# Last down-projection without an accumulator swap, a final norm that leaves GpSimd, and matmuls of the wide products chained in program order

## The chip, the cores and the metric

The kernel runs on one core of a Trainium2 chip. The metric is the device time of one execution in microseconds (us), the median over several runs. The engines are TensorE (PE for matmuls, PEld for the weight loads that precede them), VectorE (DVE), ScalarE (ACT), GpSimd (POOL) and SyncE (SP), which issues most of the transfers.

## What is computed

A decoder trunk of two mixer layers and two feed-forward layers on 256 tokens of width 2048, in float32, with a final RMSNorm. The part that the change touches most is the last feed-forward layer and the norm behind it:

```python
def conv_ffn(h, w_up, conv_w, w_down):
    up = h @ w_up
    g, u = jnp.split(up, [D_FF], axis=-1)      # D_FF = 5632
    g = causal_dwconv(g, conv_w)               # width 3
    return (jax.nn.silu(g) * u) @ w_down

...
    x = x + conv_ffn(h, ffn_w_up[l], ffn_conv_w[l], ffn_w_down[l])
return rmsnorm(x, norm_final)
```

Layer 0 has dilated attention beside a convolution module, layer 1 attention with forget gates; both end in an output projection that is added to x.

## The kernel before

**Weights.** Every product streams its weights through `stream` (lines 79 to 98): SP loads 1 MB into a `raw` buffer (three of them); ACT rounds a chunk of 128x1024 into `whi`, and DVE subtracts it from `raw` to give the remainder `wlo`. There are four `whi` and four `wlo` buffers. A product of float32 numbers is made of the products of rounded parts and remainders. One chunk holds two blocks of 128 rows of k for 512 columns.

**Wide products.** `panel_b` (line 100) gives 512 output features by 256 tokens: four PSUM banks, one for each 128 features (m), and for each block of k a matmul of `whi` with both parts of x side by side (512 columns, L111), then one of `wlo` with the main part (256 columns, L115). With `wide=False`, in layer 0's mixer, the first is split in two (L113, L114). All panels take their banks from the pool `pacc` of five in rotation; a pool `pms` of three ("misc") serves attention, norms and transposes. So a panel's first bank is free at its start, and its other three are those of the panel before, which DVE and ACT empty first: `whole` (L121, L123) for gate panels g, up panels u and q and k; `add_x` (L214, L215) where the product is added to x: ob (layer 0's output), d0 (first down-projection) and oc (layer 1's output).

**Order.** The program is emitted in one order, and a scheduler with a timeline of its own fixes each engine's instruction order: it takes what is ready in that timeline, by priority. In the order that it makes, a panel's matmuls mostly alternate between L111 and L115, with runs of L111 in places. `tc.high_priority` moves the casts and subtractions ahead.

**The last projection.** The second feed-forward layer goes in two groups of up panels (gi = 0 and 1). For gi = 0, `down1` (line 618) transposes x back to token rows (`x_back`) and adds its products with `panel_a` (`mm_a`, L127 to L129: three matmuls of 512 columns for each block of k). For gi = 1 it closes both PSUM pools and opens a pool `pl` of eight banks, one for each 512 columns i and token tile t:

```python
        ps_scope.close()
        pl = ctx.enter_context(tc.tile_pool(name="pl", bufs=1, space=bass.MemoryType.PSUM))
        acc = [[pl.tile([P, 512], F32, name=f"acc_e{i}{t}") for t in range(2)] for i in range(4)]
```

These tiles are called acc_e. Of its 20 blocks of k, the first 18 go to both token tiles alike; the last two are split, token tile 0 first, then token tile 1. After each token tile `finish_rows` (L660) adds the four banks to o (`add_o`, L616), squares on ACT (L664), sums, takes the reciprocal root (`rsqrt_cols`, L157 to L165), multiplies by the gain `gb` on POOL (L669), scales by the root on DVE (L673) and ACT (L675), and stores (L676).

Of the kernel before, what the change touches and what calls it, by code (L numbers as in the profile page):

```python
# [34 lines left out]

P_AG, P_Q, P_K, P_V, P_O = 2.4, 2.6, 2.6, 2.4, 3.4
ACT_TAPS = (1,)
AHEAD, BEHIND, TAIL = 400, 300, 60


@with_exitstack
def trunk(ctx, tc, a):
# [6 lines left out]
    ps_scope = ctx.enter_context(ExitStack())  # L49
    pacc = ps_scope.enter_context(tc.tile_pool(name="pacc", bufs=5, space=bass.MemoryType.PSUM))  # L50
    pms = ps_scope.enter_context(tc.tile_pool(name="pms", bufs=3, space=bass.MemoryType.PSUM))

    def misc(name):
        return pms.tile([P, 512], F32, tag="misc", name=name)
# [24 lines left out]
    def stream(src_of, nk, width, name, dk=4, room=None):  # L79

        half = KC * 512 // width
        for c in range(0, nk, dk * 512 // width):
            n = dk * 512 // width
            raw = wp.tile([P, 2 * KC * 512], F32, tag="raw", name=f"raw_{name}_{c}", bufs=3)
            rv = raw[:, :n * width].rearrange("p (k c) -> p k c", k=n)
            loads.append(nc.sync.dma_start(out=rv, in_=src_of(c, n)))
            for h in range(0, n, half):
                if room is None:
                    hi = wp.tile([P, half, width], F32R, tag="whi", name=f"whi_{name}_{c + h}")
                    lo = wp.tile([P, half, width], F32R, tag="wlo", name=f"wlo_{name}_{c + h}")  # L90
                else:
                    hi = room.tile([P, half, width], F32R, tag="gp", name=f"whi_{name}_{c + h}", bufs=2)
                    lo = room.tile([P, half, width], F32R, tag="cv", name=f"wlo_{name}_{c + h}", bufs=2)
                with tc.high_priority(offset=AHEAD):
                    S.copy(hi, rv[:, h:h + half, :])  # L95
                    last = V.tensor_tensor(out=lo, in0=rv[:, h:h + half, :], in1=hi.bitcast(F32), op=ALU.subtract)  # L96
                fill_in(last)
                yield list(range(c + h, c + h + half)), hi, lo

    def panel_b(src_of, x2, kts, name, order=(0, 1, 2, 3), dk=4, wide=True):  # L100

        acc = {m: pacc.tile([P, 512], F32, tag="acc", name=f"acc_{name}_{m}") for m in order}
        for ks, hi, lo in stream(src_of, len(kts), P * len(order), name, dk):
            for m in order:
                ms = slice(m * P, (m + 1) * P)
                for j, k in enumerate(ks):
                    x = x2(kts[k])
                    if wide:  # L110
                        PE.matmul(acc[m], hi[:, j, ms], x.rearrange("p a t -> p (a t)"), start=k == 0, stop=False)  # L111
                    else:
                        PE.matmul(acc[m][:, :T], hi[:, j, ms], x[:, 0, :], start=k == 0, stop=False)  # L113
                        PE.matmul(acc[m][:, :T], hi[:, j, ms], x[:, 1, :], start=False, stop=False)  # L114
                    PE.matmul(acc[m][:, :T], lo[:, j, ms], x[:, 0, :], start=False, stop=k == len(kts) - 1)  # L115
        return acc

    def whole(out, acc, name):
# [35 lines left out]
    def rsqrt_cols(ps, scale, name, n=2):  # L154

        v = wk.tile([P, n], F32, tag="rs_v", name=f"v_{name}")
        V.tensor_scalar(out=v, in0=ps, scalar1=scale, scalar2=EPS, op0=ALU.mult, op1=ALU.add)  # L157
        r = wk.tile([P, n], F32, tag="rs_r", name=f"r_{name}")
        S.activation(r, v, AF.Sqrt)
        V.reciprocal(out=r, in_=r)  # L160
        t = wk.tile([P, n], F32, tag="rs_t", name=f"t_{name}")
        V.tensor_tensor(out=t, in0=r, in1=r, op=ALU.mult)
        V.tensor_tensor(out=t, in0=t, in1=v, op=ALU.mult)
        V.tensor_scalar(out=t, in0=t, scalar1=-0.5, scalar2=1.5, op0=ALU.mult, op1=ALU.add)
        V.tensor_tensor(out=r, in0=r, in1=t, op=ALU.mult)  # L165
        return r
# [451 lines left out]
    def down1(gi, w_dn, k0, kts, g2, fp):  # L618
        if gi == 0:
# [28 lines left out]
        for i in range(4):  # L648
            for got in part(i, at, KC):
                for t in range(2):  # L650
                    rows(i, t, at, *got)
        at = n - KC
# [7 lines left out]
    def finish_rows(acc, t):  # L660
        for i in range(4):
            cs = slice(512 * i, 512 * (i + 1))
            add_o(acc[i][t], t, i)
            S.activation(junk[:, 512 * (i % 2):512 * (i % 2) + 512], o[:, t, cs], AF.Square, accum_out=fs[:, t, i:i + 1])  # L664
        V.reduce_sum(out=sf[:, t:t + 1], in_=fs[:, t, :], axis=AX.X)
        rf = rsqrt_cols(sf[:, t:t + 1], 1.0 / D, f"fin{t}", 1)
        for i in range(4):
            cs = slice(512 * i, 512 * (i + 1))
            G.tensor_tensor(out=o[:, t, cs], in0=o[:, t, cs], in1=gb[:, cs], op=ALU.mult)  # L669
        for i in range(4):  # L670
            cs = slice(512 * i, 512 * (i + 1))
            if i % 2 == 0:
                V.tensor_scalar(out=o[:, t, cs], in0=o[:, t, cs], scalar1=rf, scalar2=None, op0=ALU.mult)  # L673
            else:
                S.activation(o[:, t, cs], o[:, t, cs], AF.Copy, scale=rf)  # L675
            nc.sync.dma_start(out=a["out"][t * P:(t + 1) * P, cs], in_=o[:, t, cs])  # L676

    ffn(1, ssq2, down1)

# [60 lines left out]
```

## Time and profile before

| what | before |
|---|---|
| median of 3 runs | 2239.58 us (2237.7 to 2240.04) |
| the profiled execution's own time | 2240.73 us |
| its span, first to last instruction | 2238.9 us |
| mean granted TensorE clock | 0.996 of full speed |
| PE busy | 2213.6 us, 99% of the span |
| DVE, ACT, POOL busy | 1493.3, 1120.4, 26.0 us |
| moved by DMA | 414.08 MB, mean 185 GB/s |

Times in rows are in us from the span's start. A row of the timeline gives start, duration, engine, line, operation, the tile written and the tiles read; "x3" means three merged instructions, and brackets hold the idle time of the engine before it with what ended it. Matmuls overlap in their pipeline, so the distance between two starts is what a matmul costs, not its duration.

### The profile page before, as it was taken

The numbers are of one execution on the slowest core, as the hardware profiler recorded it, in microseconds if no ns is written. First come the engines' busy times: TensorE is split into PE (matmuls) and PEld (weight loads), VectorE is DVE, ScalarE is ACT, GpSimd is POOL, SyncE is SP. The second block draws the span as 40 slices with busy tenths as digits, with TensorE's granted clock in tenths as the row PEclk, the third lists the DMA queues.
The fourth block names the chain that finished last, engine by engine and source line by source line (L and its number), as shares of the span: only waits on it lengthen the run. The fifth ranks groups of instructions, "written<-read, shape, count | busy, mean of one in ns | idle before, by whom it ended". The sixth has DMA issues, their size and how long they took to land.

```text
span 2238.9 us, 31976 instructions
## 1 busy us (share of the span) xinstructions
PE 2213.6 (99%) x12778; PEld 1944.4 (87%) x12778; DVE 1493.3 (67%) x2280; ACT 1120.4 (50%) x1579; POOL 26.0 (1%) x58
## 2 busy tenths in 40 slices
PE   8999999999999999999999999999999999999997
PEld 8999988888888888888888888888888888888886
DVE  6999988767754577666655555677666644676644
ACT  6567665544443445444554554455544433454433
POOL 0000000000000000000000000000000000000001
PEclk9999999999999999999999999999999999999999
DMA  8544445555555555555544444555555555555453
GB/s 289 182 183 169 162 177 188 188 188 189 188 188 188 188 188 189 188 189 188 189 173 170 170 170 170 188 183 193 188 188 188 188 190 195 188 185 188 168 194 122
DMA packets 60806, 414.08 MB, mean 185 GB/s; under 512 B 7296, under 2 KB 8000, under 8 KB 12272
## 3 DMA queue, kind: packets, MB, share of 16 engines
q1 hardware_dynamic: 59904, 410.72, 51.2%
q8 instruction: 100, 1.64, 0.3%
q10 hardware_dynamic: 144, 1.05, 0.1%
q0 software_dynamic: 608, 0.26, 0.0%
q14 instruction: 50, 0.41, 0.0%
HBM read 409.84 MB, written 2.10 MB: 184 GB/s over the span
## 4 chain that ended last, share of the span: by engine, by line
PE 97%; DMA 1%; DVE 1%; ACT 0%; SPq 0%; issue 0%; ACTq 0%; DVEq 0%
PE acc_g L111 15%; PE acc_u L111 14%; PE acc_g L115 7%; PE acc_u L115 7%; PE acc_d L111 7%; PE acc_d L115 4%; PE acc_oc L111 3%; PE acc_k L111 3%; PE acc_q L111 3%; PE acc_q L115 2%; PE acc_k L115 2%; PE acc_d L127 2%; PE acc_d L129 2%; PE acc_v L128 2%; PE acc_v L129 2%; PE acc_v L127 2%
## 5 line engine op out<-in xcount | busy, mean ns | idle before, releaser
L111 PE MATMUL acc_g<-xs,whi_g 128*128 128x512 f32 x1408 | 493.0, 397 | 0.0
L111 PE MATMUL acc_u<-xs,whi_u 128*128 128x512 f32 x1408 | 481.9, 395 | 0.0
L115 PE MATMUL acc_g<-xs,wlo_g 128*128 128x256 f32 x1408 | 388.7, 280 | 0.0
L115 PE MATMUL acc_u<-xs,wlo_u 128*128 128x256 f32 x1408 | 370.0, 279 | 0.0
L96 DVE TENSOR_TENSOR wlo_g<-raw_g,whi_g 128x1024 fp32r<-128x1024 f32 x176 | 215.2, 1224 | 166.3 <-ACT whi_g L95 166.3
L111 PEld LDWEIGHTS acc_g<-xs,whi_g 128*128 128x128 f32 x1408 | 262.6, 188 | 60.5
L111 PEld LDWEIGHTS acc_u<-xs,whi_u 128*128 128x128 f32 x1408 | 260.1, 188 | 52.7
L95 ACT CAST whi_u<-raw_u 128x1024 fp32r<-128x1024 f32 x176 | 185.1, 1052 | 239.6 <-PE acc_u L111 122.0
L96 DVE TENSOR_TENSOR wlo_u<-raw_u,whi_u 128x1024 fp32r<-128x1024 f32 x176 | 213.3, 1222 | 116.2 <-ACT whi_u L95 116.2
L95 ACT CAST whi_g<-raw_g 128x1024 fp32r<-128x1024 f32 x176 | 184.9, 1052 | 198.3 <-PE acc_u L111 93.3
L96 DVE TENSOR_TENSOR wlo_d<-raw_d,whi_d 128x1024 fp32r<-128x1024 f32 x136 | 166.5, 1225 | 161.4 <-ACT whi_d L95 161.2
L115 PEld LDWEIGHTS acc_u<-xs,wlo_u 128*128 128x128 f32 x1408 | 265.0, 188 | 9.0
L115 PEld LDWEIGHTS acc_g<-xs,wlo_g 128*128 128x128 f32 x1408 | 265.6, 189 | 3.0 <-DVE wlo_g L96 0.2
L95 ACT CAST whi_d<-raw_d 128x1024 fp32r<-128x1024 f32 x136 | 143.0, 1051 | 207.2 <-PE acc_d L111 118.8
L111 PE MATMUL acc_d<-hp,whi_d 128*128 128x512 f32 x704 | 245.2, 394 | 0.0
L115 PE MATMUL acc_d<-hp,wlo_d 128*128 128x256 f32 x704 | 194.4, 283 | 0.0
L111 PEld LDWEIGHTS acc_d<-hp,whi_d 128*128 128x128 f32 x704 | 131.3, 188 | 28.8
L115 PEld LDWEIGHTS acc_d<-hp,wlo_d 128*128 128x128 f32 x704 | 132.4, 188 | 1.9
L115 PE MATMUL acc_q<-xs,wlo_q 128*128 128x256 f32 x384 | 106.0, 283 | 0.0
L115 PE MATMUL acc_k<-xs,wlo_k 128*128 128x256 f32 x384 | 105.8, 281 | 0.0
L111 PE MATMUL acc_q<-xs,whi_q 128*128 128x512 f32 x256 | 90.6, 396 | 0.0
L96 DVE TENSOR_TENSOR wlo_e<-raw_e,whi_e 128x1024 fp32r<-128x1024 f32 x40 | 48.9, 1225 | 60.4 <-ACT whi_e L95 60.4
(305 smaller groups left out, 4178.0 us busy)
## 6 DMA issues: line engine op xcount, KB each, us to landing
raw_g<-in_ffn_w_up SPq DMA_DIRECT2D x88, 1024.0 KB, 4.7
raw_u<-in_ffn_w_up SPq DMA_DIRECT2D x88, 1024.0 KB, 4.8
raw_d<-in_ffn_w_down SPq DMA_DIRECT2D x68, 1024.0 KB, 4.7
raw_q<-in_od_w_in SPq DMA_DIRECT2D x16, 1024.0 KB, 4.8
raw_k<-in_od_w_in SPq DMA_DIRECT2D x16, 1024.0 KB, 4.8
raw_v<-in_od_w_in SPq DMA_DIRECT2D x16, 1024.0 KB, 4.7
raw_oc<-in_od_w_out SPq DMA_DIRECT2D x16, 1024.0 KB, 4.8
raw_e<-in_ffn_w_down SPq DMA_DIRECT2D x16, 1024.0 KB, 4.8
```

The costliest lines, as they stand in the source:

```text
L95: S.copy(hi, rv[:, h:h + half, :])
L96: last = V.tensor_tensor(out=lo, in0=rv[:, h:h + half, :], in1=hi.bitcast(F32), op=ALU.subtract)
L111: PE.matmul(acc[m], hi[:, j, ms], x.rearrange("p a t -> p (a t)"), start=k == 0, stop=False)
L115: PE.matmul(acc[m][:, :T], lo[:, j, ms], x[:, 0, :], start=False, stop=k == len(kts) - 1)
L127: PE.matmul(o, xh, hi, start=first, stop=False)
L128: PE.matmul(o, xh, lo, start=False, stop=False)
L129: PE.matmul(o, xl, hi, start=False, stop=last)
```

## The change

1. The pools `pacc` and `pms` stay open to the end. The eight acc_e tiles come from them: three from "misc", five from `pacc`.
2. In the last projection the first 16 blocks of k go to both token tiles alike, and the last four are split by token tile. Their eight chunks must all stay in SBUF; buffers come from tiles that are dead by then (gate and conv tiles, one `hp` buffer, the four ordinary buffers, one `raw` buffer).
3. The final norm: after each 512 columns the sum is added, squared on ACT, and for three of four multiplied by `gb` on DVE instead of POOL; the fourth is multiplied by root and gain in one DVE instruction. In `rsqrt_cols` two DVE multiplications become one instruction when there is one column. The order of the four output blocks becomes 1, 0, 3, 2. The priority of `finish_rows` (`TAIL`) goes.
4. Each matmul of a wide product depends on the one before it (no semaphore, only order), through the whole kernel: `in_order`.

```diff
+    issued = [None]
+    def in_order(*args, **kw):
+        i = PE.matmul(*args, **kw).ins
+        if issued[0] is not None:
+            tc.add_manual_dep(i, issued[0].name, mybir.DependencyInfo(mybir.DependencyClass.NoSync, mybir.DependencyReason.DATA),
+                              reason="order of a product's matmuls")
+        issued[0] = i
...
+        mm = in_order if wide else PE.matmul
...
-        V.tensor_tensor(out=t, in0=r, in1=r, op=ALU.mult)
-        V.tensor_tensor(out=t, in0=t, in1=v, op=ALU.mult)
+        if n == 1:
+            V.scalar_tensor_tensor(out=t, in0=r, scalar=v, in1=r, op0=ALU.mult, op1=ALU.mult)
...
-        ps_scope.close()
-        pl = ctx.enter_context(tc.tile_pool(name="pl", bufs=1, space=bass.MemoryType.PSUM))
-        acc = [[pl.tile([P, 512], F32, name=f"acc_e{i}{t}") for t in range(2)] for i in range(4)]
+        acc = [[None, None] for i in range(4)]
+        for b, (i, t) in enumerate((i, t) for i in range(4) for t in range(2)):
+            acc[i][t] = misc(f"acc_e{i}{t}") if b < 3 else pacc.tile([P, 512], F32, tag="acc", name=f"acc_e{i}{t}")
...
-        last = [next(part(i, at, KC, room=fp if i > 1 else None)) for i in range(4)]
-        for t in range(2):
-            for i in range(4):
-                rows(i, t, at, *last[i])
-            with tc.high_priority(offset=TAIL * t):
-                finish_rows(acc, t)
+        rooms = [from_gate] * 2 + [from_hidden] + [from_weights] * 4 + [from_raw]
+        at = n - 4
+        last = [list(part(i, at, 4, room=lambda nm: rooms.pop(0)(nm))) for i in range(4)]
+        for t in range(2):
+            for i in range(4):
+                for got in last[i]:
+                    rows(i, t, at, *got)
+                add_o(acc[i][t], t, i)
+                cs = slice(512 * i, 512 * (i + 1))
+                S.activation(junk[:, 512 * (i % 2):512 * (i % 2) + 512], o[:, t, cs], AF.Square, accum_out=fs[:, t, i:i + 1])
+                if i < 3:
+                    V.tensor_tensor(out=o[:, t, cs], in0=o[:, t, cs], in1=gb[:, cs], op=ALU.mult)
+            V.reduce_sum(out=sf[:, t:t + 1], in_=fs[:, t, :], axis=AX.X)
+            rf = rsqrt_cols(sf[:, t:t + 1], 1.0 / D, f"fin{t}", 1)
+            for i in (1, 0, 3, 2):
+                cs = slice(512 * i, 512 * (i + 1))
+                if i == 3:
+                    V.scalar_tensor_tensor(out=o[:, t, cs], in0=o[:, t, cs], scalar=rf, in1=gb[:, cs], op0=ALU.mult, op1=ALU.mult)
+                elif i == 1:
+                    V.tensor_scalar(out=o[:, t, cs], in0=o[:, t, cs], scalar1=rf, scalar2=None, op0=ALU.mult)
+                else:
+                    S.activation(o[:, t, cs], o[:, t, cs], AF.Copy, scale=rf)
+                nc.sync.dma_start(out=a["out"][t * P:(t + 1) * P, cs], in_=o[:, t, cs])
```

`from_gate`, `from_hidden`, `from_weights` and `from_raw` are small new functions that each return a pair of views for `whi` and `wlo` in one of the buffers named under 2.

## Rows read from the trace of the kernel before

**Rows 1.** The page, busy time, share of the span and instructions of the engines.
```profile
PE 2213.6 (99%) x12778; PEld 1944.4 (87%) x12778; DVE 1493.3 (67%) x2280; ACT 1120.4 (50%) x1579; POOL 26.0 (1%) x58
```

**Rows 2.** Waits of PE over the span: total, times, longest.
```profile
...
PE bc_n L174 <- DVE dg_n L172: 2.0, 1, 2.0
PE acc_ob L111 <- DVE y L453: 1.4, 1, 1.4
```

**Rows 3.** Timeline of PE where the last projection begins.
```profile
2110.68 0.28 PE L115 MATMUL acc_u<-xs,wlo_u 128*128 128x256 f32 x1
2114.27 0.79 PE L127 MATMUL acc_e<-whi_e,hp 128*128 128x512 f32 x1 [3.32 <-DVE half_u L123]
...
2120.27 0.39 PE L129 MATMUL acc_e<-whi_e,hp 128*128 128x512 f32 x1
...
2120.96 0.39 PE L129 MATMUL acc_e<-whi_e,hp 128*128 128x512 f32 x1
```

**Rows 4.** Windows there: length, busy time by engine, then granted TensorE clock (PEclk), DMA.
```profile
2110.90:2114.20 3.30, 0.06 (x1) 0.00 (x0) 3.30 (x9) 2.21 (x5) 0.00 (x0) 0.86 0.25 104
2114.20:2118.00 3.80, 3.73 (x9) 2.96 (x10) 1.45 (x5) 1.89 (x3) 0.00 (x0) 0.50 0.73 276
```

**Rows 5.** Timeline of DVE before the last projection begins: third chunk of its weights.
```profile
2109.19 1.23 DVE L96 TENSOR_TENSOR wlo_e<-raw_e,whi_e 128x1024 fp32r<-128x1024 f32 x1 [1.55 <-ACT whi_e L95]
```

**Rows 6.** Timeline of PE, last matmul of token tile 0's first bank, and of all.
```profile
2217.09 0.39 PE L129 MATMUL acc_e<-whi_e,hp 128*128 128x512 f32 x1
...
2226.80 0.39 PE L129 MATMUL acc_e<-whi_e,hp 128*128 128x512 f32 x1
```

**Rows 7.** Timeline of DVE in the final norm.
```profile
2217.52 0.69 DVE L616 TENSOR_TENSOR o<-acc_e,o 128x512 f32<-128x512 f32 x1 [1.27 <-PE acc_e L129]
...
2225.24 1.20 DVE L162 TENSOR_TENSOR t_fin<-r_fin 128x1 f32<-128x1 f32 x1
...
2229.43 0.68 DVE L616 TENSOR_TENSOR o<-acc_e,o 128x512 f32<-128x512 f32 x1
...
2231.77 0.51 DVE L162 TENSOR_TENSOR t_fin<-r_fin 128x1 f32<-128x1 f32 x1
2232.31 0.16 DVE L163 TENSOR_TENSOR t_fin<-t_fin,v_fin 128x1 f32<-128x1 f32 x1
...
2232.96 0.88 DVE L673 TENSOR_SCALAR o<-o,r_fin 128x512 f32<-128x512 f32 x2
```

**Rows 8.** Timeline of POOL in the final norm.
```profile
2221.35 6.30 POOL L669 TENSOR_TENSOR o<-o,xT 128x512 f32<-128x512 f32 x5 [1.01 <-ACT xT L664]
```

**Rows 9.** Windows over one gate panel each, of layer 0 and of layer 1.
```profile
439.50:462.00 22.50, 22.50 (x130) 19.55 (x129) 13.85 (x21) 11.01 (x16) 0.00 (x0) 1.00 0.55 190
...
1886.90:1909.10 22.20, 22.20 (x130) 19.57 (x129) 11.06 (x12) 9.43 (x11) 0.00 (x0) 1.00 0.55 194
```

**Rows 10.** Timeline of PE inside an up panel of layer 1.
```profile
1606.11 0.40 PE L111 MATMUL acc_u<-xs,whi_u 128*128 128x512 f32 x1
...
1608.94 0.40 PE L111 MATMUL acc_u<-xs,whi_u 128*128 128x512 f32 x1
...
1609.29 1.11 PE L111 MATMUL acc_u<-xs,whi_u 128*128 128x512 f32 x4
```

**Rows 11.** Timeline of DVE in the same up panel.
```profile
1605.14 1.22 DVE L96 TENSOR_TENSOR wlo_u<-raw_u,whi_u 128x1024 fp32r<-128x1024 f32 x1
```

**Rows 12.** Timeline, PE's first matmul of an up panel, DVE emptying the gate panel's banks.
```profile
462.04 0.40 PE L111 MATMUL acc_u<-xs,whi_u 128*128 128x512 f32 x1
...
461.52 1.08 DVE L123 TENSOR_TENSOR gp<-acc_g,half_g 128x256 f32<-128x256 f32 x3
```

**Rows 13.** Timeline, PE's first matmul of the last ob panel, DVE emptying a bank before.
```profile
337.60 0.40 PE L111 MATMUL acc_ob<-y,whi_ob 128*128 128x512 f32 x1
...
342.14 0.41 DVE L215 TENSOR_TENSOR xT<-acc_ob,xT 128x256 f32<-128x256 f32 x1
```

**Rows 14.** Window behind PE's wait for dg_n, columns as in rows 4.
```profile
34.50:38.00 3.50, 3.50 (x16) 3.32 (x16) 3.50 (x6) 2.83 (x5) 0.00 (x0) 0.51 0.57 169
```

More of the change, by code (lines that the diff above doesn't have):

```diff
@@ L48, in trunk @@
     wk = ctx.enter_context(tc.tile_pool(name="wk", bufs=2))
-    ps_scope = ctx.enter_context(ExitStack())
-    pacc = ps_scope.enter_context(tc.tile_pool(name="pacc", bufs=5, space=bass.MemoryType.PSUM))
-    pms = ps_scope.enter_context(tc.tile_pool(name="pms", bufs=3, space=bass.MemoryType.PSUM))
+    pacc = ctx.enter_context(tc.tile_pool(name="pacc", bufs=5, space=bass.MemoryType.PSUM))
+    pms = ctx.enter_context(tc.tile_pool(name="pms", bufs=3, space=bass.MemoryType.PSUM))
     def misc(name):
@@ L91, in stream @@
                 else:
-                    hi = room.tile([P, half, width], F32R, tag="gp", name=f"whi_{name}_{c + h}", bufs=2)
-                    lo = room.tile([P, half, width], F32R, tag="cv", name=f"wlo_{name}_{c + h}", bufs=2)
+                    hi, lo = room(f"{name}_{c + h}")
                 with tc.high_priority(offset=AHEAD):
@@ L110, in panel_b @@
                     if wide:
-                        PE.matmul(acc[m], hi[:, j, ms], x.rearrange("p a t -> p (a t)"), start=k == 0, stop=False)
+                        mm(acc[m], hi[:, j, ms], x.rearrange("p a t -> p (a t)"), start=k == 0, stop=False)
                     else:
-                        PE.matmul(acc[m][:, :T], hi[:, j, ms], x[:, 0, :], start=k == 0, stop=False)
-                        PE.matmul(acc[m][:, :T], hi[:, j, ms], x[:, 1, :], start=False, stop=False)
-                    PE.matmul(acc[m][:, :T], lo[:, j, ms], x[:, 0, :], start=False, stop=k == len(kts) - 1)
+                        mm(acc[m][:, :T], hi[:, j, ms], x[:, 0, :], start=k == 0, stop=False)
+                        mm(acc[m][:, :T], hi[:, j, ms], x[:, 1, :], start=False, stop=False)
+                    mm(acc[m][:, :T], lo[:, j, ms], x[:, 0, :], start=False, stop=k == len(kts) - 1)
         return acc
@@ L161, in rsqrt_cols @@
         t = wk.tile([P, n], F32, tag="rs_t", name=f"t_{name}")
[L162 to L163 removed]
+        if n == 1:
+            V.scalar_tensor_tensor(out=t, in0=r, scalar=v, in1=r, op0=ALU.mult, op1=ALU.mult)
+        else:
+            V.tensor_tensor(out=t, in0=r, in1=r, op=ALU.mult)
+            V.tensor_tensor(out=t, in0=t, in1=v, op=ALU.mult)
         V.tensor_scalar(out=t, in0=t, scalar1=-0.5, scalar2=1.5, op0=ALU.mult, op1=ALU.add)
@@ L646, in down1, with from_gate, from_hidden @@
                         rows(i, t, at, *got)
-        at = n - 4
-        for i in range(4):
-            for got in part(i, at, KC):
-                for t in range(2):
-                    rows(i, t, at, *got)
-        at = n - KC
-        last = [next(part(i, at, KC, room=fp if i > 1 else None)) for i in range(4)]
+        def from_gate(nm):
+            return [fp.tile([P, KC, 512], F32R, tag=tag, name=f"{w}_{nm}", bufs=2) for tag, w in (("gp", "whi"), ("cv", "wlo"))]
+        def from_hidden(nm):
+            both = fp.tile([P, 4, 2, T], F32R, tag="hp", name=f"wboth_{nm}", bufs=6).rearrange("p a b t -> p (a b t)")
+            return [both[:, 1024 * h:1024 * (h + 1)].rearrange("p (k c) -> p k c", k=KC) for h in range(2)]
@@ new lines, in from_weights, with from_raw @@
+        def from_weights(nm):
+            return [wp.tile([P, KC, 512], F32R, tag=w, name=f"{w}_{nm}") for w in ("whi", "wlo")]
+        def from_raw(nm):
+            both = wp.tile([P, 2 * KC * 512], F32, tag="raw", name=f"wboth_{nm}", bufs=3).bitcast(F32R)
+            return [both[:, 1024 * h:1024 * (h + 1)].rearrange("p (k c) -> p k c", k=KC) for h in range(2)]
+        rooms = [from_gate] * 2 + [from_hidden] + [from_weights] * 4 + [from_raw]
+        at = n - 4
+        last = [list(part(i, at, 4, room=lambda nm: rooms.pop(0)(nm))) for i in range(4)]
```

20 lines of the change are left out of this document (2 added, 18 removed).

## The prediction, made before the changed kernel ran

> **What bounds the kernel now.** I read the page first: PE is busy for 99% of the span [rows 1], so another engine matters only where it makes PE wait, or behind PE's last matmul. The list of PE's waits comes next. It is short: besides a start-up wait and the two of [rows 2], its longest is the 3.32 us in front of the last projection [rows 3]. The windows show that this wait costs twice: behind it the granted clock is 0.50, the lower level of 1.2 GHz, instead of 1.00 [rows 4]. Then the tail, by the timelines of PE, DVE and POOL: the last matmul starts at 2226.80 [rows 6], the scaling by the last root at 2232.96 [rows 7], and the span ends at 2238.9. Of those 12 us some are DVE's queue and not the norm's own chain. Last I compared the distance between matmuls in panels of one shape, because edit 4 touches all of them: 44 gate and up panels of 64 pairs of L111 and L115 make 2,816 pairs, so a nanosecond a pair is 2.8 us.
>
> **Pools left open.** The wait goes to DVE's L123, the last emptying of the last up panel, because the new pool needs all eight banks [rows 3]. After the change the first three acc_e tiles are "misc" banks, which nobody uses by then, the fourth is the fifth bank of `pacc`, and the four banks of the up panel are wanted only by i = 2 and 3. Two rounds of 24 matmuls (i = 0 and 1, 0.23 us each) lie before that, 11 us, while the emptying takes 3.3 us. The weights are there: the third chunk's remainder is done at 2110.42 [rows 5]. So the first matmul starts one L115 spacing behind 2110.68 (a pair's 0.35 us [rows 10] less 0.23, so 0.12) instead of at 2114.27: 3.47 us won. With PE never idle, the clock stays up. From 2114.27 to 2120.27 there are 14 spacings (6.00 us); at the later 0.23 us (three in 2120.27 to 2120.96 [rows 3]) they take 3.20: 2.80 us won.
>
> The Trainium skill (TensorE: Matmul & The Clock Gate, "Why this matters for your kernels") says the same of idle gaps between bursts, which bring the engine back to the lower level; but this trace shows it behind a wait of only 2.0 us as well [rows 2], clock 0.51 [rows 14], sooner than the page's advice suggests. By the page a new stall of 2 us would cost 2 us, by the trace up to 2 or 3 us more.
>
> **Early token tile.** The same 480 matmuls run, so PE's time is unchanged. What could stall is the supply: in token tile 0's pass a chunk serves six matmuls only, 1.4 us, while DVE needs 1.23 a chunk and 1.4 more for each two chunks (add and gain multiply, 0.69 each, the second priced by the add's row [rows 7]). It is hidden by being early: the first three chunks use dead buffers and need no PE release; the next four take the buffers of the last four ordinary chunks, of which the last comes free when the pass begins and is wanted 8 us later; the eighth takes a `raw` buffer whose own chunks are cast long before. ACT stands in order behind those casts, but only squares of token tile 0 queue there. I cost it at nothing; if the cover failed, one chunk's cast and subtraction, about 2.3 us, would show as a PE wait.
>
> **Norm.** In the first pass DVE's add starts 0.43 us behind the bank's last matmul (2217.09 [rows 6], 2217.52 [rows 7]). The very last add starts 2.63 us behind (2226.80, 2229.43). It stands in DVE's queue behind token tile 0's root, where two one-column multiplications took 1.20 us each [rows 7] while POOL was multiplying by the gain [rows 8]; alone, such a multiplication takes 0.16. After the change token tile 0 is finished under 11 us of token tile 1's matmuls and POOL is idle: 2.20 us won. On the last chain the 0.51 us multiplication (again beside POOL) becomes 0.16, 0.35 won, and merging it with its successor saves one step of 0.20 (2232.31 to the next start). Adding or multiplying a fourth block costs nothing there, since block 3 gets root and gain in one DVE instruction; it may take 0.69 instead of half of 0.88, and since the third store waits for it, 0.25 us is its bound; I take nothing, because ACT's block before it is stored first. Moving token tile 0's four stores earlier takes them off SP's queue before the last four are due. Sum: 2.75 us. The stores and their landing, from 2232.96 to the end 5.9 us, stay.
>
> **Strict order.** This removes nothing from PE's list of waits, since there is nothing there but ob's 1.4 us (a data wait that stays). It can act in three ways.
>
> First, waits for remainders. The scheduler had moved `whi` matmuls ahead in runs of four (1609.29 [rows 10]), as if `wlo` were late; in the trace that chunk's `wlo` was finished at 1606.36 [rows 11], 2.9 us earlier. Alternating there costs nothing.
>
> Second, waits for banks at a panel's start. Banks 2, 3 and 4 are wanted 0.7, 1.4 and 2.1 us behind the panel's first matmul (two blocks of k at 0.35). Between gate and up panel the three are emptied by 462.60, that is 0.56 us behind 462.04 [rows 12]: no wait. In ob, where DVE has a backlog, the third of them is free at 342.55, 4.95 us behind 337.60 [rows 13]: up to 2.9 us of waiting at this boundary, and I estimate less at the two beside it, 4.7 in all. But that backlog comes partly from chunks that were held longer because the order ran ahead on one bank. Between 0 and 4.7 I take 1.5.
>
> Third, the spacing itself. One gate panel takes 22.5 us, another of the same 130 matmuls 22.2 [rows 9], both with PE busy throughout. A pair costs 0.354 us in a strictly alternating stretch (eight from 1606.11 to 1608.94 [rows 10]), which makes 22.65 for 64 pairs, so strict alternation alone does not decide it; the trace shows two spacings that last for whole stretches and change where the order is broken. With the order unbroken, a stretch keeps what it entered with. Over 44 gate and up panels, all at 22.2 against 22.5 gives up to 13 us less; all at 22.65, some 7 us more. I take 1.5 us less, near the middle, because the one gate panel that starts behind a non-wide product is of the short kind. The second and third cancel.
>
> **Sum.** 3.47 + 2.80 + 2.75 = 9.0 us, from strict order 0. The profiled execution took 2240.73, which becomes 2231.7; it lies 1.15 above the median of the runs, 2239.58, so the median becomes **2230.6 us**.
>
> **Rivals.**
>
> *Short spacing throughout.* The order is never broken, and the panels settle at 22.2. For it: the panel of layer 1 [rows 9]. Against: the alternating stretch at 0.354 [rows 10]. With 10 of the 13 us it gives 2239.58 - 9 - 10 = 2220.
>
> *Strict order eats most of it.* Long spacing in most panels (+6), or ob's waits in full (+4.7, with the clock lost +7): 2235 to 2238, within 0.2% of before (4.5 us, about what a measurement of this kernel can tell from no change).
>
> *The early start does not come.* The first acc_e matmul waits for another thing (a "misc" bank, a cast behind the emptying on ACT): 6.3 of the 9 us are lost, 2236.9. Against it stand the finished weights [rows 5].
>
> *Slower.* Bank waits at every one of the 69 wide panels' starts (44 gate and up, 8 first down, 8 query and key, 8 output panels and the gate logits). It decides from 13.5 us in all, 0.2 us a panel. If the third bank came 0.3 us late in each, PE would wait 21 us: 2239.58 - 9 + 21 = 2252. Against it: 1.5 us of margin at gate and up panels [rows 12]; for it: ob [rows 13]. The Trainium skill (same page, "A second HAM failure mode: psum-queue depth-cycling") describes this: cycling through PSUM banks makes PE idle briefly between groups, and the clock swings. In this trace five banks are cycled and the clock is 1.00 in both panels of rows 9; whether strict order changes that no run here shows yet.
>
> **Chances.** Forecast, 2226 to 2235: 0.60. Short spacing: 0.13. Eaten by strict order: 0.15. No early start: 0.06. Slower: 0.06. So faster by over 0.2%: the first two and 0.02 of the third, 0.75; within 0.2%: 0.19; slower: 0.06. Leaving out the far part of the short spacing and the slower case, the range is 2221 to 2238.
>
> **What will show it.** PE's waits should list no acc_e, and the window behind 2110 a clock of 1.00. The last add should start 0.4 us behind the last matmul and the scaling 3.0 us later (now 3.5). PE waits on DVE's L214 or L215 lines at ob would confirm the bank waits; gate panels of 22.2 or 22.65 us decide the spacing. I am wrong if waits for banks appear at gate and up panels, or if the last projection waits for a cast.

## The result: 2227.9 us, with the gain in two places

| | median, us | runs, us |
|---|---|---|
| before, beside it on the same chip | 2239.64 | 2237.7 to 2240.04 (4) |
| after | 2227.9 | 2225.25 to 2229.79 (4) |

The ratio is 0.995, its 95% interval 0.9938 to 0.9961: 11.7 us faster, against 9.0 forecast, and inside the range of 2221 to 2238. The profiled execution after took 2227.58, its span 2225.8. Engines first (the line of the page that answers to [rows 1]):

```profile
PE 2206.7 (99%) x12778; PEld 1944.7 (87%) x12778; DVE 1490.9 (67%) x2284; ACT 1118.0 (50%) x1579; POOL 15.6 (1%) x50
```

PE has the same 12778 matmuls and is still the bound, but is busy 6.9 us less. The view of PE's waits, as in [rows 2]:

```profile
PE acc_ag L122 <- ACT whi_ag L93: 6.7, 1, 6.7
PE acc_ob L102 <- DVE y L465: 1.6, 2, 1.4
PE bc_n L186 <- DVE dg_n L184: 1.6, 1, 1.6
PE acc_ag L124 <- DVE wlo_ag L94: 0.4, 2, 0.2
```

The list has no acc_e any more, and no wait for a bank anywhere; ob's wait has become two. The start of the last projection in PE's timeline, and the windows behind it (columns as in [rows 4]), which answer to [rows 3, 4]:

```profile
2106.72 0.28 PE L102 MATMUL acc_u<-xs,wlo_u 128*128 128x256 f32 x1
2106.84 0.39 PE L136 MATMUL acc_e<-whi_e,hp 128*128 128x512 f32 x1
2107.07 0.39 PE L137 MATMUL acc_e<-wlo_e,hp 128*128 128x512 f32 x1
```

```profile
2106.80:2110.80 4.00, 4.00 (x20) 3.30 (x19) 4.00 (x10) 3.21 (x6) 0.00 (x0) 1.00 0.34 121
2110.80:2114.80 4.00, 4.00 (x19) 3.30 (x18) 2.54 (x5) 2.92 (x5) 0.00 (x0) 1.00 0.65 254
```

The first acc_e matmul starts one spacing (0.12 us) behind the last up matmul, the next 0.23 later, and the clock is 1.00 from the first stretch on. The tail, PE's last matmul and DVE's steps behind it, beside [rows 6, 7]:

```profile
2216.62 0.40 PE L138 MATMUL acc_e<-wboth_e,hp 128*128 128x512 f32 x1
```

```profile
2217.05 0.69 DVE L628 TENSOR_TENSOR o<-acc_e,o 128x512 f32<-128x512 f32 x1 [0.52 <-PE acc_e L138]
...
2219.41 0.22 DVE L172 SCALAR_TENSOR_TENSOR t_fin<-r_fin,v_fin 128x1 f32<-128x1 f32 x1
...
2220.05 0.48 DVE L695 TENSOR_SCALAR o<-o,r_fin 128x512 f32<-128x512 f32 x1
```

The last add now stands 0.43 us behind the last matmul (2.63 before) and the scaling 3.00 behind the add (3.53 before). POOL has no work in the final norm.

The rest of the difference is found by laying both timelines side by side: the length of each stretch, from its first matmul to that of the next.

| stretch | before, us | after, us | difference |
|---|---|---|---|
| start to ob's first matmul | 303.64 | 304.17 | +0.53 |
| ob (four output panels of layer 0) | 45.48 | 47.66 | +2.18 |
| gate and up panels 0 to 5, layer 0 | 269.84 | 267.46 | -2.38 |
| down panels, first group | 134.87 | 135.18 | +0.31 |
| gate and up panels 6 to 10, layer 0 | 224.18 | 222.01 | -2.17 |
| down panels, second group | 112.33 | 112.71 | +0.38 |
| layer 1: attention, then output panels | 392.16 | 392.07 | -0.09 |
| gate and up panels 0 to 5, layer 1 | 272.55 | 271.86 | -0.69 |
| down (token-major), layer 1 | 131.85 | 131.85 | 0 |
| gate and up panels 6 to 10, layer 1, with the wait | 227.38 | 221.87 | -5.51 |
| last projection, first to last matmul | 112.53 | 109.78 | -2.75 |
| last matmul to the end | 12.13 | 9.18 | -2.95 |

Together -13.1 us of span. The end of the program gives 9.17 of it: 3.47 of the wait (within the -5.51), 2.75 and 2.95. Of the other 3.96, the +0.53 of the start is not the change's: PE has the same 2216 matmuls in the same order there in every kernel, and the fourteen profiles of this document take between 301.93 and 304.48 us for it (304.17 and 302.12 in two of the changed kernel). The rest, some 4.5 us, comes from strict order, in which gains in gate and up panels (-7.28 without the wait) stand against losses elsewhere. Windows over one gate panel, one up panel and one panel with a foreign piece in it (columns as in [rows 4]) show what the gains are:

```profile
441.84:464.02 22.18, 22.18 (x131) 19.56 (x130) 13.63 (x21) 11.03 (x16) 0.00 (x0) 1.00 0.54 190
1907.16:1929.34 22.18, 22.18 (x130) 19.56 (x129) 17.49 (x27) 10.68 (x13) 0.11 (x1) 1.00 0.52 185
1504.70:1528.61 23.91, 23.91 (x143) 20.94 (x142) 17.72 (x27) 13.41 (x17) 0.11 (x1) 1.00 0.47 168
```

Where [rows 9] had 22.5 us, layer 0 now has 22.18 as well: 64 pairs of 346.7 ns. The third window is the first up panel of layer 1, where twelve transposes of tb stand between the pairs; behind them its pairs run at 353.3.

### The profile page after: what moved, and what is told of

The parts are those of the page before. It is cut to its first block, busy times and chain, and to the rows that moved or that the text cites. A ratio compares the mean times of both kernels' runs of the same rounds, so it can differ in the third digit from the quotient of the medians.

```text
span 2225.8 us, 31945 instructions
## 1 busy us (share of the span) xinstructions
PE 2206.7 (99%) x12778; PEld 1944.7 (87%) x12778; DVE 1490.9 (67%) x2284; ACT 1118.0 (50%) x1579; POOL 15.6 (1%) x50
## 4 chain that ended last, share of the span: by engine, by line
PE 98%; DMA 1%; ACT 1%; DVE 0%; SPq 0%; issue 0%; ACTq 0%; DVEq 0%
PE acc_g L102 22%; PE acc_u L102 22%; PE acc_d L102 11%; PE acc_oc L102 4%; PE acc_q L102 4%; PE acc_k L102 4%; PE acc_ob L102 2%; PE acc_d L136 2%; PE acc_d L138 2%; PE acc_v L137 2%; PE acc_v L138 2%; PE acc_v L136 2%; PE acc_d L137 2%; PE acc_e L137 2%; PE acc_e L136 2%; PE acc_e L138 2%
## 5 line engine op out<-in xcount | busy, mean ns | idle before, releaser
L102 PE MATMUL acc_u<-xs,whi_u 128*128 128x512 f32 x1408 | 489.8, 392 | 0.0
L102 PE MATMUL acc_g<-xs,wlo_g 128*128 128x256 f32 x1408 | 394.1, 280 | 0.0
L102 PE MATMUL acc_u<-xs,wlo_u 128*128 128x256 f32 x1408 | 393.4, 279 | 0.0
L102 PE MATMUL acc_d<-hp,wlo_d 128*128 128x256 f32 x704 | 199.1, 283 | 0.0
L102 PE MATMUL acc_oc<-y,whi_oc 128*128 128x512 f32 x256 | 90.3, 395 | 0.0
L102 PE MATMUL acc_k<-xs,whi_k 128*128 128x512 f32 x256 | 88.9, 391 | 0.0
L94 DVE TENSOR_TENSOR wlo_v<-raw_v,whi_v 128x1024 fp32r<-128x1024 f32 x48 | 58.7, 1222 | 45.1 <-ACT whi_v L93 44.4
```

The costliest lines, as they stand in the source:

```text
L102: i = PE.matmul(*args, **kw).ins
```

## Experiments

"Short" and "long" below are the two spacings of a pair, 346.7 and 353.3 ns; a gate or up panel of 64 pairs takes 22.18 or 22.62 us with the one or the other. A "break" is a chunk in which whi and wlo matmuls don't alternate throughout. "Before" in the table is the kernel before, run beside the experiment on the same chip.

| kernel | median, us (runs) | before, us | ratio (95%) |
|---|---|---|---|
| written order dropped from after | 2230.12 (2229.6 to 2231.89) | 2238.35 | 0.9963 (0.995 to 0.9975) |
| written order alone | 2238.64 (2234.59 to 2242.37) | 2238.35 | 0.9997 (0.9988 to 1.0006) |
| after, ob left to the scheduler | 2228.6 (2223.98 to 2229.68) | 2238.35 | 0.9952 (0.994 to 0.9965) |
| open pools alone | 2233.48 (2232.66 to 2235.25) | 2238.35 | 0.9979 (0.997 to 0.9988) |
| after, runs of four | 2232.33 (2230.84 to 2233.42) | 2239.59 | 0.9968 (0.9956 to 0.9981) |
| after, one wlo out | 2232.0 (2230.84 to 2232.69) | 2239.59 | 0.9966 (0.9954 to 0.9979) |
| after, gain on POOL | 2229.61 (2226.09 to 2231.27) | 2239.59 | 0.9956 (0.9942 to 0.9969) |
| after, ob by block | 2231.67 (2226.76 to 2232.48) | 2239.59 | 0.9959 (0.9946 to 0.9972) |
| after again | 2226.27 (2223.67 to 2229.97) | 2239.16 | 0.9942 (0.993 to 0.9955) |
| after, four breaks | 2232.38 (2229.97 to 2242.5) | 2239.16 | 0.9976 (0.996 to 0.9991) |
| after, eight breaks | 2230.32 (2228.4 to 2231.71) | 2239.16 | 0.996 (0.9947 to 0.9972) |
| after, order in gate and up alone | 2228.31 (2223.59 to 2228.91) | 2239.16 | 0.9946 (0.9934 to 0.9959) |

### Taking the parts apart

First, the changed kernel without its written order:

```diff
-        mm = in_order if wide else PE.matmul
+        mm = PE.matmul
```

> The change with the order of the wide products left free again, so only its last projection and norm. Theory A (the last projection and norm win what they were priced at, 9.0 us and the order's share is separate): 2239.6 - 9.1 = 2230.5 us, PE's first acc_e without a wait and at clock 1.00, spacing of pairs as before (mean near 0.350 us), ob again about 45.5 us long. Rival B (the order chain does nothing, the other edits give the whole 11.7 us by shifting the schedule): 2228 us.

It gained 8.2 us (2238.35 to 2230.12) where the prediction's sum for these parts is 9.0; the interval of the ratio allows 5.6 to 11.2. In its trace the stretch with the wait takes 223.90 us instead of 227.38, the last projection 109.78 and the tail 9.19: the same three terms, now with gate and up panels as before.

Next, the pools alone, in the kernel before:

```diff
-        ps_scope.close()
-        pl = ctx.enter_context(tc.tile_pool(name="pl", bufs=1, space=bass.MemoryType.PSUM))
...
+            acc[i][t] = misc(f"acc_e{i}{t}") if b < 3 else pacc.tile([P, 512], F32, tag="acc", name=f"acc_e{i}{t}")
```

> The kernel before with the PSUM pools left open and nothing else. Theory A: the 3.3 us wait and the half clock behind it go, 2239.6 - 6.2 = 2233.4 us; the last add still starts 2.6 us behind the last matmul. Rival (another wait takes its place, a cast or a bank): PE shows a wait at acc_e, 2236 us or more.

It gained 4.9 us, with an interval of 2.7 to 6.7 that holds the predicted 6.27. The timelines of PE and DVE at its end show that the tail is untouched:

```profile
2221.36 0.39 PE L128 MATMUL acc_e<-whi_e,hp 128*128 128x512 f32 x1
```

```profile
2221.01 1.21 DVE L162 TENSOR_TENSOR t_fin<-t_fin,v_fin 128x1 f32<-128x1 f32 x1
...
2223.97 0.68 DVE L615 TENSOR_TENSOR o<-acc_e,o 128x512 f32<-128x512 f32 x1
```

The last add is again 2.61 us late, behind a root whose one-column multiplication takes 1.21 us. So pools and tail are separate terms.

Then the written order alone, in the kernel before:

```diff
+        mm = in_order if wide else PE.matmul
...
-                        PE.matmul(acc[m], hi[:, j, ms], x.rearrange("p a t -> p (a t)"), start=k == 0, stop=False)
+                        mm(acc[m], hi[:, j, ms], x.rearrange("p a t -> p (a t)"), start=k == 0, stop=False)
...
```

> The kernel before with only the order chain of the wide products. Theory A: pairs at 0.347 us in gate and up panels instead of 0.350 on average, about -7.7 us there, and about +2.7 us at ob and at the start: 2235 us, gate panels 22.2 us. Rival B (the chain does nothing): 2239.6 us. Rival C (it costs bank waits): over 2241 us.

No difference in the median, and runs 7.8 us apart. Windows over one panel in each of the four stretches of its profile:

```profile
417.17:439.35 22.18, 22.18 (x130) 19.56 (x129) 17.49 (x27) 10.68 (x13) 0.11 (x1) 1.00 0.54 190
797.37:819.99 22.62, 22.62 (x131) 19.60 (x130) 13.63 (x21) 11.01 (x16) 0.00 (x0) 1.00 0.51 186
1621.60:1643.79 22.19, 22.19 (x131) 19.39 (x129) 13.63 (x21) 11.01 (x16) 0.00 (x0) 1.00 0.54 194
1930.94:1953.13 22.19, 22.19 (x130) 19.57 (x129) 13.63 (x21) 11.03 (x16) 0.00 (x0) 1.00 0.55 192
```

The second stretch is long in all its ten panels: 226.25 us, against 222.01 in after, with the same order. So the written order as such does not bring 22.18; a stretch can be long in one profile and short in another. The changed kernel once more, unaltered, tells whether that belongs to the kernel:

> The changed kernel itself once more. Theory A (with the order unbroken each of the four stretches of gate and up panels runs wholly at 346.7 or wholly at 353.3 ns a pair, and which one a stretch enters with is settled anew in each run, in layer 0 at least): runs spread over 4 us or more, since the two stretches of layer 0 (768 and 640 pairs) are worth 5.1 and 4.3 us each; median 2227 to 2231. Rival B (the levels belong to the kernel): runs within 2 us of 2228, and the profile again all at 22.2 us a panel.

The runs spread over 6.3 us, as theory A has it. The spread alone does not speak for it, though: this profile's span is 2.6 us shorter than that of after's first profile, and 2.05 of these lie in the start, where the order is the same. The profile, however, came out short in both stretches of layer 0, as after's first one had, so this kernel alone didn't show both levels. The kernels with an unbroken order taken together do: in seven profiles (after, after again, order alone, ob free, gain on POOL, ob by block, gate and up alone) the first stretch of layer 0 is long once, its second three times. In the first stretch the level settles late: the norm's matmuls ss_f and bc_f stand in its first panel, and in five of the seven the level changed behind one of these. In layer 1 the same panels had the same level in all seven: the two behind twelve transposes each long, the one behind eight transposes (23.09 us with them) and all later ones short.

### What changes the level

> The changed kernel, except that in the third chunk of each of the 22 gate panels the order is broken once, in the way in which up panels of the kernel before showed it: four whi matmuls in a row, then wlo and whi by turns, and two wlo at the end of it. Theory A (the spacing of a stretch has two levels, 346.7 and 353.3 ns a pair, and is set where the order is broken; this way of breaking it leads to the short one): all 44 gate and up panels take 22.2 us in each run, the median is 2226 or less and the runs lie within 3 us of each other. Rival B (the level is not set by breaks of the order): as the changed kernel, 2228 with runs some 5 us apart, and panels of both lengths in the profile or none different from the changed kernel's. If the break only swaps the levels, about half of the panels would be long: 2233.

The edit, in each gate panel's third chunk (H is a whi matmul, l a wlo, with the number of the pair); behind the four whi matmuls it has two wlo in a row three times, as up panels of the kernel before have in their fifth and sixth chunks:

```diff
+            if name[0] == "g" and ks[0] == 4:
+                seq = [(int(c[1]), c[0]) for c in "H0 H1 H2 H3 l0 H4 l1 l2 H5 l3 l4 H6 l5 l6 H7 l7".split()]
```

The other form of break, one wlo put at the chunk's end:

```diff
+            if name[0] == "g" and ks[0] == 4:
+                seq = [seq[0]] + seq[2:] + [seq[1]]
```

> The changed kernel, except that in the third chunk of each of the 22 gate panels one wlo matmul is put at the chunk's end (whi whi at its start, wlo wlo at its end), the other way in which the kernel before broke the order, at panel starts. Theory A (such a break takes a stretch to the long spacing of 353.3 ns a pair): most gate and up panels at 22.6 us instead of 22.2, up to 8 us more: 2231 to 2236. Theory C (each break swaps the levels, so panels alternate): the mean of the two, about 2232, with levels changing once a layer block in the profile. Rival B (breaks don't matter): 2228, panels as in the changed kernel.

Theory A fell in both: neither form leads always to the short spacing or always to the long one. What mostly held is the other case named in each, that a break swaps the levels: its estimates were 2233 and 2232, the medians are 2232.33 and 2232.0. Windows over four successive up panels of the kernel with one wlo out, with one break between each and the next:

```profile
417.88:440.06 22.18, 22.18 (x130) 19.39 (x129) 17.49 (x27) 10.66 (x13) 0.10 (x1) 1.00 0.55 191
462.56:485.18 22.62, 22.62 (x131) 19.62 (x129) 17.55 (x27) 10.66 (x13) 0.10 (x1) 1.00 0.52 184
507.52:529.70 22.18, 22.18 (x130) 19.40 (x129) 17.48 (x27) 10.66 (x13) 0.11 (x1) 1.00 0.54 186
552.20:574.82 22.62, 22.62 (x131) 19.62 (x129) 17.54 (x27) 10.66 (x13) 0.10 (x1) 1.00 0.53 184
```

PE is busy throughout at clock 1.00 in all four; only the level alternates. Over both kernels, 36 of the 44 breaks changed it. With swaps the levels average out, as they did in the kernel before; the runs spread over 2.6 and 1.9 us, less than with the unbroken order (6.3), but the kernel before, which swaps too, spreads over 5 to 6 in nine and eleven runs, so the spread is no proof.

If a break swaps a level that then lasts, four breaks should be enough to turn the whole kernel's panels long. The edit is the last one, for four panels:

```diff
+            if name in ("g0_0", "g0_6", "g1_0", "g1_6") and ks[0] == 4:
+                seq = [seq[0]] + seq[2:] + [seq[1]]
```

> The changed kernel, except that one wlo matmul is put at its chunk's end in the third chunk of the first gate panel of each of the four stretches: four chunks of 352. Theory A (a break of that form swaps the two levels, and the level stays until the next): what is short becomes long. 2720 pairs lie behind the four breaks, 6.67 ns each, 18.1 us if all four stretches enter short as in the changed kernel's profile; if those of layer 0 enter either way, 9.1 us from layer 1 and 0 to 9 from layer 0: 2237 to 2246, as slow as the kernel before or slower. Rival B (breaks don't set the level, or four of them are too few to matter): 2228 to 2230.

The median, 2232.38, is short of the 2237 to 2246 expected, and the runs spread over 12.5 us. Windows over a panel of the first, second and fourth stretch of its profile:

```profile
461.58:484.19 22.61, 22.61 (x131) 19.62 (x129) 17.54 (x27) 10.66 (x13) 0.11 (x1) 1.00 0.52 185
845.54:868.16 22.62, 22.62 (x131) 19.60 (x129) 13.63 (x21) 11.01 (x16) 0.00 (x0) 1.00 0.51 185
...
1911.65:1933.84 22.19, 22.19 (x130) 19.40 (x129) 17.50 (x27) 10.66 (x13) 0.11 (x1) 1.00 0.54 189
```

Both stretches of layer 0 are long, 8.9 us more than in after's; layer 1 is unmoved. Only the second stretch is long by the break. The first entered long (353.7 ns a pair in its second chunk), the break took it to short, and behind bc_f, still in its first panel, it is long again. In the third stretch, too, other matmuls stand behind the break (ss_f, bc_f, the transposes tb), and the level behind those was the one that it is in every profile with unbroken order here. In the fourth the break changed nothing. The same panels with a second break, in the sixth chunk:

```diff
-            if name in ("g0_0", "g0_6", "g1_0", "g1_6") and ks[0] == 4:
+            if name in ("g0_0", "g0_6", "g1_0", "g1_6") and ks[0] in (4, 10):
```

> As the kernel with four swapped chunks, but with a second chunk of the same first panels, the sixth, broken in the same way: eight chunks. Theory A (each break swaps): the second one undoes the first, the stretches go on as they entered, and the time is that of the changed kernel, 2227 to 2231. Rival C (a break puts a stretch on the long spacing, whatever it had): as with four chunks, 2237 to 2246. Rival B (the breaks cost by themselves): twice the loss of the four.

At 2230.32 it is where theory A has it; a doubled loss or a lasting long level (2237 and more) is excluded. That the median is there is partly luck, since only one of the four stretches went as theory A says. Its second stretch shows the mechanism in one panel (means of eight pairs, from their starts): 346.6 ns ahead of the first break, 352.4 to 354 between the two, 346.8 behind the second. Its fourth shows the exception again: the first break changed nothing, the second took the stretch to long, 225.87 us instead of 221.87. In the first stretch the same happened, but bc_f took it back to short.

So a break can move the level and usually does. What the exceptions have in common can be read from the distances of the pairs, taken to the nanosecond: there are two kinds of short. In the first, pairs of 347, 347 and 346 ns follow each other; in the second, pairs of 350 and 343 take turns. (A long stretch runs 350, 361, 349.) Both shorts have the same mean, but in the second the durations in PE's timeline take turns as well. In the kernel with one wlo out, ahead of a break that changed nothing (fourth stretch, first gate panel):

```profile
1890.89 0.28 PE L102 MATMUL acc_g<-xs,wlo_g 128*128 128x256 f32 x1
1891.01 0.39 PE L102 MATMUL acc_g<-xs,whi_g 128*128 128x512 f32 x1
1891.24 0.28 PE L102 MATMUL acc_g<-xs,wlo_g 128*128 128x256 f32 x1
```

and ahead of one that led to long (second stretch, second gate panel):

```profile
801.84 0.27 PE L102 MATMUL acc_g<-xs,wlo_g 128*128 128x256 f32 x1
801.96 0.40 PE L102 MATMUL acc_g<-xs,whi_g 128*128 128x512 f32 x1
802.19 0.28 PE L102 MATMUL acc_g<-xs,wlo_g 128*128 128x256 f32 x1
802.31 0.39 PE L102 MATMUL acc_g<-xs,whi_g 128*128 128x512 f32 x1
```

The four kernels with breaks have 56 broken chunks in their profiles. All 11 that were entered in the first short led to the second short, so that the level did not change; all 21 entered in the second short led to long; of 24 entered in long, 21 led to a short. Seven of the eight exceptions among the 44 are of the first sort. This is a reading of four profiles, and no kernel was made to test it.

### ob

> The change with the chain taken off the four ob panels alone. Theory A (the chain holds ob's second matmul pair behind a y that is not ready, and PE's clock falls there): ob back to about 45.5 us from 47.7, no half clock near 305 us, 2227.9 - 2.2 = 2225.7 us. Rival (the fall of the clock there is chance, not the order): 2227.9 us, half clock still there in some runs.

```diff
-        mm = in_order if wide else PE.matmul
+        mm = in_order if wide and not name.startswith("ob") else PE.matmul
```

ob is back at 45.46 us in the profile, but a new wait of 0.8 us makes the stretch behind it 1.13 longer than in after:

```profile
PE acc_ob L120 <- DVE y L465: 1.4, 1, 1.4
PE bc_n L186 <- DVE dg_n L184: 1.2, 1, 1.2
PE acc_g L102 <- DVE xT L227: 0.8, 1, 0.8
```

The first gate panel now waits for a bank that DVE is still emptying. The median did not tell it from after: the 1.1 us that are left are small beside the 4 to 5 that a stretch of layer 0 is worth.

With the written order kept, but blocks of k outside:

```diff
+            if name.startswith("ob"):
+                pairs = [(m, j) for j in range(len(ks)) for m in order]
```

> The changed kernel, with the ob panels still held in the written order, but with the blocks of k outside and the four banks inside, so that each block of y is used by all four banks before the next is needed. Theory A (ob's loss of 2.2 us in the changed kernel is not the order's being held but its needing block k+1 of y after one pair instead of four; PE then waits twice and its clock falls): ob takes 45.5 us as before, one wait of 1.4 us, no half clock, no new wait at the first gate panel: 2225.7. Rival B (holding any order costs ob its 2 us, for instance by waits for banks): ob stays at 47.7 and the time at 2227.9.

Theory A fell. ob takes 48.27 us, and its waits are of another kind:

```profile
PE acc_ob L102 <- DVE xT L233: 2.7, 3, 0.9
PE acc_ob L102 <- DVE y L471: 1.4, 1, 1.4
...
PE acc_g L102 <- DVE xT L233: 0.5, 1, 0.5
```

The second wait for y is gone and the clock stays up, as expected; but a panel that needs all four banks in its first 1.4 us waits 0.9 us for DVE's emptying at three boundaries. These are the bank waits that the prediction bounded from [rows 13]; this order has them, the changed kernel's doesn't. Its first stretch of gate and up panels was long besides (272.65 us), which is more than its whole distance from after.

What ob's 2.2 us are in the changed kernel is read from PE's timeline there:

```profile
304.17 0.50 PE L102 MATMUL acc_ob<-y,whi_ob 128*128 128x512 f32 x1 [1.37 <-DVE y L465]
304.51 0.27 PE L102 MATMUL acc_ob<-y,wlo_ob 128*128 128x256 f32 x1
305.05 0.50 PE L102 MATMUL acc_ob<-y,whi_ob 128*128 128x512 f32 x1 [0.27 <-DVE y L465]
305.39 0.37 PE L102 MATMUL acc_ob<-y,wlo_ob 128*128 128x256 f32 x1
```

and the window behind:

```profile
305.40:308.90 3.50, 3.50 (x13) 3.01 (x12) 2.97 (x7) 2.41 (x6) 0.00 (x0) 0.51 0.12 19
```

The second pair needs the next block of y, which isn't there; in the kernel before, four pairs on the first block came ahead of it. Behind this second wait the granted clock is 0.51, the lower level of 1.2 GHz. The written order alone is not enough for that. In the profile with four breaks, where ob is ordered in the same way and waits the same 1.37 and 0.27 us, the window at the same place reads:

```profile
303.10:306.60 3.50, 3.50 (x21) 2.95 (x21) 2.94 (x7) 3.44 (x7) 0.00 (x0) 1.00 0.10 19
```

and ob takes 45.75 us. Of eight profiles with these two waits, the clock fell in five (ob 47.5 to 47.7 us) and stayed in three (45.8 to 46.1); of five with the single wait of 1.4 it fell in none (45.5). So 0.3 to 0.6 us is the order's, and some 1.7 the clock's, in part of the executions.

Last, the order where it can win and nowhere else:

```diff
-        mm = in_order if wide else PE.matmul
+        mm = in_order if name[0] in "gu" else PE.matmul
```

> The changed kernel with the written order held in gate and up panels alone; ob, down, query, key and output panels are left to the scheduler, as in the kernel before. Theory A: ob is back at 45.5 us (2.2 less, of which a wait of 0.8 at the first gate panel may come back), first down, output and the panels between are 1.1 us shorter, gate and up panels stay at one level for each stretch: 1.5 to 3.5 us less than the changed kernel in a run of the same levels, median 2224 to 2228. Rival B (ob's and the down panels' time is not the order's): as the changed kernel.

ob took 45.46 us, the down groups 134.86 and 112.31 (0.7 less together), and the wait of 0.8 at the first gate panel is there again. Against gain on POOL, whose gate and up panels have the same levels in the profile, the span is 0.7 us shorter (2226.5 and 2227.2), less than the 1.5 expected, and 0.48 of it lies in the start and 0.09 in the tail; its median does not differ from that of after. No version here beats the changed kernel by more than runs differ.

### The norm

> The changed kernel, except that the three gain multiplications of 128x512 for each token tile are back on POOL; the early token tile stays. Theory A (the prediction's split: 2.20 us come from the early token tile, which takes the root's queue away from the last add, and only 0.35 of the norm's part from POOL's being idle): the last add still starts 0.43 us behind the last matmul, the last chain is 0 to 0.4 us longer, median 2228.0 to 2228.6. Rival B (it is VectorE instead of POOL that brings the gain): the last add starts late again, one-column multiplications take 0.5 to 1.2 us, and 2 to 3 us are lost: about 2230.5.

```diff
                 if i < 3:
-                    V.tensor_tensor(out=o[:, t, cs], in0=o[:, t, cs], in1=gb[:, cs], op=ALU.mult)
+                    G.tensor_tensor(out=o[:, t, cs], in0=o[:, t, cs], in1=gb[:, cs], op=ALU.mult)
```

Timelines of its tail, on PE, POOL and DVE:

```profile
2217.95 0.40 PE L138 MATMUL acc_e<-wboth_e,hp 128*128 128x512 f32 x1
```

```profile
2217.22 1.28 POOL L687 TENSOR_TENSOR o<-o,xT 128x512 f32<-128x512 f32 x1 [1.46 <-ACT xT L685]
```

```profile
2218.39 0.69 DVE L628 TENSOR_TENSOR o<-acc_e,o 128x512 f32<-128x512 f32 x1 [2.06 <-PE acc_e L138]
...
2220.74 0.22 DVE L172 SCALAR_TENSOR_TENSOR t_fin<-r_fin,v_fin 128x1 f32<-128x1 f32 x1
...
2221.45 0.49 DVE L695 TENSOR_SCALAR o<-o,r_fin 128x512 f32<-128x512 f32 x1
```

The last add is 0.44 us behind the last matmul, the scaling 3.06 behind the add, and the tail takes 9.27 us instead of 9.18. POOL's last multiplication ends at 2218.50, before the root begins. So which engine multiplies the first three blocks is worth 0.09 us. The rest of the tail's gain is left to finishing token tile 0 early and to the fourth block, whose multiplication no longer stands beside the root; by the timelines these are the 2.20 and the 0.53, but no run has the one without the other. The median is 1.7 above after's first one, but the profile has the second stretch of layer 0 long (226.24 us), which alone is 4.2.

## Why the prediction was right, and which term was mis-sized

**Pools left open** (3.47 + 2.80): right. The wait is gone, the start is 0.12 us behind the last up matmul, and the last projection is 2.75 us shorter because the clock never falls. Two kernels without the written order show the stretch with the wait at 223.90 us, 3.48 less than before.

**Early token tile** (0, and the condition for the next term): right. No acc_e wait appears in any kernel with it.

**Norm** (2.75): 2.95. The queue gave 2.20 as worked out, the root 0.53 against 0.55, and 0.22 more came behind the scaling. The reason for one piece was too broad: POOL need not be idle in general, as the run with the gain on POOL shows; by the timelines it is enough that nothing multiplies beside the last root.

**Strict order** (0, as -1.5 of spacing and +1.5 of bank waits): this is the mis-sized term, some -4.5 us in the profile (-3.96 with the +0.53 of the start). *Remainders*: right, no such wait. *Banks*: at the boundaries named it is 0 in this order. The +2.18 at ob come from a wait for y, 0.27 us, with a fall of the clock behind it. The prediction called ob's 1.4 us "a data wait that stays" and did not ask which data the second pair would need. *Spacing*: the two levels held in every kernel, and a level lasted through every panel without a break or foreign matmuls; "a stretch keeps what it entered with" failed where ss_f, bc_f or tb stand between the pairs, in the first panels of two of the four stretches. And -1.5 us became -7.28. The reason given for the size, one gate panel of the short kind, said nothing on where the other stretches would enter. Not priced at all: down and output panels, 1.06 us longer in written order (+0.31, +0.38, and +0.37 within the -0.09 of the table's row for layer 1).

The size is partly one of the execution. In the kernel before, the breaks make gate panels of 22.5 and up panels of 22.3 us, near the mean of the two levels; the three profiles with that order (before, order dropped, open pools alone) have the same stretches within 0.02 us, the wait aside. Without breaks each stretch of layer 0, behind its first panel, is all short or all long, worth 5.1 and 4.2 us. Both profiles of the changed kernel caught it short. Over its nine runs the median is 2227.1; without the written order it is 2230.1 on another occasion, with a kernel before that differs by under 1.3 us. So the written order is worth about 3 us here, and in the kernel before it was worth nothing that could be measured (2238.64 and 2238.35). The profiles allow both. Outside layer 0's gate and up panels it gives little: -2.73 in those of layer 1, against +0.60 in the down panels and the rest of layer 1 and +0.3 to +2.2 at ob. Layer 0's give -4.55 in after and -0.46 in order alone. That the result lies 2.7 us below the forecast is in part the luck of how layer 0's stretches came out.

**The rivals.** Short spacing throughout is what most gate and up panels did in the profile; 2220 was not reached because ob, the down and output panels gave back 3.2 us and two panels of layer 1 stayed long. Strict order eating the gain did not happen, though its ob part did. Bank waits at every panel's start appear in no kernel: PE's list has none at gate and up panels but the one of 0.5 to 0.8 us behind ob in three variants. The Trainium skill's section on cycling through PSUM banks (TensorE: Matmul & The Clock Gate, "A second HAM failure mode: psum-queue depth-cycling") speaks of a clock that swings with brief idling between groups; here the clock is 1.00 in every gate and up window shown, with five banks cycled in either order, so it did not show.

Open are two things: what settles the kind of spacing with which a stretch is entered (the second of layer 0 was entered long in three of seven profiles with unbroken order, in the first short in two, in the second short in two), and why a break or a foreign matmul changes it. No run tried to hold the level from outside.

## What to carry to other kernels

Price the end of a program by the trace: a wait there costs its length and the slower clock behind it, and what finishes the first half of the output early also takes its queue away from the last one. Where one order is to be held, hold it where it was seen to win, and ask at each stage which input the second instruction needs; an order that a scheduler bent may have been hiding a late operand. Where a stretch can take one of two lengths, as panels do here, one profile doesn't explain a median: compare the same stretch in several executions first.

## What the hardware showed that was not expected

- Two lasting spacings of the same pair of matmuls at granted clock 1.00 with PE busy throughout: 346.7 and 353.3 ns, 2% of a panel. The level lasts for over 600 pairs in unbroken order. The shorter spacing comes in two kinds of the same mean; 36 of 44 breaks changed the level, and seven of the eight that didn't were entered in the first kind and left in the second.
- The clock fell to 0.51 behind waits of 1.37 and 0.27 us, 0.5 us of work apart, in five of eight profiles, and behind one wait of 1.4 us in none of five. Ahead of that, at the start of the kernel, one profile has it behind a wait of 1.5 us, and another doesn't behind 1.6.
- The 128x512 multiplication by the gain took 1.28 us on POOL and 0.69 on DVE, yet moving it gained 0.09: its place beside the root matters, not its length.
